# The gates' token sums made during the low-rank products, in a pool of their own

## The chip, the cores and the metric

The kernel runs on one core of a Trainium2 chip. Five engines work in parallel, each through its own list of instructions in a fixed order: PE (matmul), DVE (vector), ACT (activations and casts), POOL and SP (which here only issues DMAs). They wait for each other through semaphores. The metric is the device time of one execution in microseconds; of several runs the median is taken.

## The reference

One decoder layer, float32, 512 tokens, model width 1024. What matters here:

```python
h    = rms_norm(x, norm_g)
proj = h @ w_in     # HGRN2 q, f, i, z_a (1024 each) | c_q, c_kv, k_rope (704) | z_b | two gates (2048)
f    = lb + (1 - lb) * sigmoid(hf);  k = 1 - f;  log_f = log(f)
y_a  = rms_norm(hgrn2_recurrence(silu(hq), k, hi, log_f)) * silu(hz)
y_b  = mla(c_q, c_kv, k_rope) * silu(mz)
gates  = sigmoid(glog + b_gate)                      # glog: the last 2048 columns of proj
merged = gates[:, :, 0] * (y_a @ w_proj_a) + gates[:, :, 1] * (y_b @ w_proj_b)
out    = rms_norm(x + merged @ w_out)
```

## The kernel before, in words

**Split operands.** Every large product is computed from pairs: an operand is cut into a rounded part (`hi`, a cast on ACT, line 129) and the remainder (`lo`, a subtraction on DVE, line 130), and three matmuls (hi·hi, lines 102; hi·lo, 103; lo·hi, 104) take the place of one. `hT` is the normalised input, transposed, as such a pair: 8 blocks of 128 channels by 512 tokens.

**Weights.** `load_w` (line 110) brings 512 KB into one of three `w_raw` buffers by a DMA on SP's queue, then casts and subtracts into one of four `w_hi` and four `w_lo` buffers. Behind each of the early weight loads a second DMA is issued on the same queue (`queued`, line 124): copies of blocks of later weight matrices from DRAM to DRAM, named `g_t`, `pa_t` and `out_t` in the trace.

**The stages around the change.** First the input is normalised and transposed, with the first 256 columns of the low-rank product (lines 292 to 357, an order written out by hand). Then the other 448 columns: 96 matmuls over four token tiles (lines 394 to 400). These are the wide low-rank products of the change. Then the latent vectors are scaled and transposed into `cT` (lines 401 to 430), and four pairs of heads of the HGRN2 branch follow (`hg_pair`, line 582). A pair begins with `proj_ch` for the forget columns (48 matmuls into two accumulators in PSUM), `hg_forget` for both heads, and, in the even pairs, `proj_tok` for the values (96 matmuls, four accumulators). These accumulators, and those of the low-rank product, come from one ring of three PSUM buffers, `mm_ps`: a fourth can be started only when the first of the three has been read out.

`hg_forget` (line 456) reads its accumulator with a tanh on ACT (line 460, tile `tf`). From `tf` DVE makes `f` (461), POOL makes `k` and `fr` (463, 462), then DVE a scan (465), a reciprocal back into `tf`'s buffer (466) and a product `ki` (483).

**The token sums.** The two gates' products are later computed by a Strassen scheme of blocks, whose operands are sums of blocks of `hT` over tokens and channels. `early_sums(q)` (line 813) makes four such sums for half of the channel blocks: four additions hi + lo (line 820), four subtractions (773, 777), four splits (171 on ACT, 172 on DVE), and eight stores of 256 KB to DRAM (line 827), which POOL's queue reads back for the gates' products much later (line 1043). Each half is thus 12 instructions on DVE, 4 on ACT and 8 DMAs on SP's queue. Its tiles `qr`, `qs`, `qh`, `p3`, `qn`, `kn`, `qp` come from the pool `ma_pool`, one buffer each; `qn` is used twice in a half. The first half stands in the first pair behind `hg_forget`, the second behind that pair.

**What sets the order.** Outside the stretches marked `manual_schedule` a scheduler chooses each engine's order by its own estimate of times, so text that moves changes the order of other instructions too. The memory is a stack from the left and one from the right; a pool that was closed leaves its bytes to later pools, and an instruction that first writes such bytes waits until those who used them before are done, tile by tile (`reuse_waits="tile"`). `hpool` with `hT` is the left stack's bottom. `hgrn`, the pool of `hg_forget`'s tiles, is on the right stack and reaches down to the very end of `hpool`; `fr`, `gh`, `asb`, `tf`, `f`, `k`, `pr`, `ft`, `ki` are its lowest tiles, in this order.

Of the kernel before, what the change touches and what calls it, by code (L numbers as in the profile page):

```python
# [9 lines left out]
F32 = mybir.dt.float32  # L10
F32R = mybir.dt.float32r
# [3 lines left out]
ALU = mybir.AluOpType  # L15
# [3 lines left out]
P = 128  # L19
# [19 lines left out]
def hybrid_layer(ctx: ExitStack, tc: tile.TileContext, a):  # L39
    nc = tc.nc  # L40
# [11 lines left out]
    dram = ctx.enter_context(tc.tile_pool(name="dram", bufs=1, space=bass.MemoryType.DRAM))  # L52
# [116 lines left out]
    def split(hi, lo, src):  # L169

        nc.scalar.copy(hi, src)
        nc.vector.tensor_tensor(lo, src, hi.bitcast(F32), op=ALU.subtract)
# [34 lines left out]
    hT = [hpool.tile([P, KD, S], F32R, f"hT{i}") for i in range(2)]  # L207
# [181 lines left out]
    nc.vector.tensor_scalar(c1n[:], lb[:], 0.5, -0.5, op0=ALU.mult, op1=ALU.add)  # L389
    nc.vector.tensor_scalar(c2[:], lb[:], 0.5, 0.5, op0=ALU.mult, op1=ALU.add)  # L390

    for t2, ps in enumerate(c_ps):
        nc.scalar.copy(c_sb[:, 2 * t2 : 2 * t2 + 2, 0:256], ps[:].rearrange("p (t c) -> p t c", t=2))
    c_second += [load_c2(j) for j in range(2, 4)]
# [187 lines left out]
    def hg_pair(pair, in_forget=None, in_query=None, before_gate=None, last=None):  # L582
        cc, hs = pair * 256, (2 * pair, 2 * pair + 1)
        pf = proj_ch(w_in, COL_F + cc, hT)
        kk = [hg_forget(h, pf[i], None if i else in_forget) for i, h in enumerate(hs)]
        if pair:
            step()
        else:
            early_sums(kh[0])
        def gate():  # L590
            pz = proj_ch(w_in, COL_ZA + cc, hT)
            zz = [z_tile() for _ in hs]
            for i in range(2):
                silu2(zz[i][:], pz[i][:])
            return zz

        if pair % 2 == 0:
            for t in range(NT):
                v_sb[t] = hw.tile([P, 512], F32, f"v{t}")
            proj_tok(w_in, COL_I + cc, hT, lambda t, ps: nc.scalar.copy(v_sb[t][:], ps[:]))  # L600
        else:
            zz = gate()
        pq = proj_ch(w_in, COL_Q + cc, hT)
        qq = [hg_query(h, pq[i], kk[i][0], None if i else in_query) for i, h in enumerate(hs)]
        step()
        kts = [hg_turned(k[5]) for k in kk]
        sts = [hg_states(h, kts[i], kk[i][1], v_sb) for i, h in enumerate(hs)]
        if before_gate:
            before_gate()
        if pair % 2 == 0:  # L610
            zz = gate()
        def scores():
            return hg_scores([(h, kk[i][2:5] + qq[i][0:2]) for i, h in enumerate(hs)])

        def outs(aa):
            on = [hg_out(h, aa[i], sts[i], qq[i][2], v_sb) for i, h in enumerate(hs)]
            step()
            return on

        def gated(on):  # L620
            for i, h in enumerate(hs):
                hg_gate(h, on[i], zz[i])

        if last:
            return last(scores, outs, gated)
        gated(outs(scores()))
# [137 lines left out]
        nc.vector.tensor_tensor(yb[:, h], ops[:], z[:], op=ALU.mult)  # L764


    kh = [slice(0, 2), slice(2, 4)]
    half_t = [slice(0, 256), slice(256, 512)]
    blocks = lambda t: (t[:, 0:4, half_t[0]], t[:, 4:8, half_t[0]], t[:, 0:4, half_t[1]], t[:, 4:8, half_t[1]])
    TERMS = ((0, 0), (1, 1), (0, 1), (1, 0))  # L770

    def minus(out, x, y):
        nc.vector.tensor_tensor(out, x, y, op=ALU.subtract)

    def minus_minus(out, x, y):

        nc.vector.scalar_tensor_tensor(out, x, -1.0, y, op0=ALU.mult, op1=ALU.subtract)

    class BlockSums:

# [27 lines left out]
    gate_w = [BlockSums(f"g{b}", w_in[:, COL_G + b * D : COL_G + b * D + D]) for b in range(2)]  # L808
    pa_w = BlockSums("pa", a["w_proj_a"][0])
    out_w = BlockSums("out", a["w_out"][0])  # L810
    h_dram = [[dram.tile([P, 4, 256], F32, name=f"h{n}{i}") for i in range(2)] for n in range(1, 5)]

    def early_sums(q):

        E = lambda tag: ma_pool.tile([P, 2, 256], F32, tag)[:]
        h11, h12, h21, h22 = zip(*[[b[:, q] for b in blocks(t)] for t in hT])

        def whole(tag, hl):
            out = E(tag)
            nc.vector.tensor_tensor(out, hl[0].bitcast(F32), hl[1].bitcast(F32), op=ALU.add)  # L820
            return out

        def keep(n, tag, src):
            hl = Pair(ma_pool.tile([P, 2, 2, 256], F32R, tag)[:])
            split(*hl, src)
            for i in range(2):
                nc.sync.dma_start(h_dram[n - 1][i][:, q], hl[i].bitcast(F32))

        e22, e21, e11, e12 = whole("qr", h22), whole("qs", h21), whole("qh", h11), whole("p3", h12)
        minus(e22, e22, e21)  # L830
        keep(1, "qn", e22)
        minus_minus(e22, e22, e11)
        keep(2, "kn", e22)
        minus(e21, e11, e21)
        keep(3, "qp", e21)
        minus_minus(e12, e12, e22)
        keep(4, "qn", e12)

    adds = [(gate_w[0], 0), (gate_w[0], 2), (gate_w[1], 0), (gate_w[0], 1), (gate_w[1], 2), (gate_w[0], 3), (gate_w[1], 1),
            (pa_w, 0), (gate_w[1], 3), (pa_w, 2), None, (pa_w, 1), (out_w, 0), (pa_w, 3), (out_w, 2), (out_w, 1), (out_w, 3)]  # L840
# [1 line left out]
    def step():  # L842
        if adds and last_pool[0]:
            x = adds.pop(0)
            if x:
                x[0].add(x[1])
# [3 lines left out]

    for pair in range(H // 2 - 1):
        hg_pair(pair)
        if pair == 0:
            early_sums(kh[1])
    early = []

    def first_scores():
# [450 lines left out]
```

## Time and profile before

| | |
|---|---|
| median of 3 runs | 606.26 us (606.16 to 606.81) |
| the profiled execution, its own time | 606.53 us |
| its span, first to last instruction | 604.7 us |
| mean granted clock of PE | 0.996 |
| busy: PE, DVE, ACT, POOL | 595.2, 445.2, 283.0, 148.3 us |
| DMA | 115.34 MB, mean 191 GB/s |

A row of the time line gives start, duration, engine, line, operation, out<-in, shapes, count and, in brackets, the idle time ahead of it and what ended that. A row of the groups gives busy time and mean duration in ns behind the first bar, idle time behind the second. A matmul's row is longer than its share of PE, since matmuls overlap; the distance of two starts is what one costs.

### The profile page before, as it was taken

How to read it: one execution, taken by the hardware profiler on the slowest of the kernel's cores; microseconds unless marked ns; L12 is line 12 of the kernel's file. 1: busy time of each engine (PE TensorE's matmuls, PEld its weight loads, DVE VectorE, ACT ScalarE, POOL GpSimd, SP SyncE). 2: the span in 40 equal slices, each digit the busy share in tenths (PEclk: the TensorE clock that was granted, in tenths of full speed). 3: DMA queues.
4: the chain of work that ended last, by engine and by line, in shares of the span. 5: the costliest groups of instructions: out<-in, count | busy, mean ns of one | idle time of the engine just before them, and what ended most of it. 6: DMA issues, size and time to landing. Idle time of an engine off the chain costs nothing.

```text
span 604.7 us, 8828 instructions
## 1 busy us (share of the span) xinstructions
PE 595.2 (98%) x3198; PEld 501.5 (83%) x3198; DVE 445.2 (74%) x689; ACT 283.0 (47%) x517; POOL 148.3 (25%) x253
## 2 busy tenths in 40 slices
PE   9999999999999999999999999999999999999994
PEld 6998888888888888888888888888888888888883
DVE  7717989599764548959767776778878878466795
ACT  7555245333313342436545554456557764153553
POOL 3107322254350237415245540400000000000003
PEclk9999999999999999999999999999999999999998
DMA  8449479997969967582369676888666656366313
GB/s 281 159 137 345 155 220 370 318 223 169 239 152 253 232 194 155 112 186 76 62 153 175 147 159 154 222 289 244 192 187 204 204 182 188 123 233 257 102 36 139
DMA packets 73036, 115.34 MB, mean 191 GB/s; under 512 B 7561, under 2 KB 37663, under 8 KB 72993
## 3 DMA queue, kind: packets, MB, share of 16 engines
q1 hardware_dynamic: 63740, 90.99, 47.2%
q0 software_dynamic: 8336, 22.55, 20.2%
q10 hardware_dynamic: 916, 1.25, 0.6%
q8 instruction: 25, 0.41, 0.3%
q14 instruction: 19, 0.15, 0.1%
HBM read 106.38 MB, written 39.85 MB: 242 GB/s over the span
## 4 chain that ended last, share of the span: by engine, by line
PE 89%; DVE 4%; DMA 3%; ACT 2%; issue 1%; POOL 1%; SPq 0%; POOLq 0%; ACTq 0%; DVEq 0%
PE mm_ps L102 19%; PE mm_ps L104 19%; PE mm_ps L103 19%; PE ax_ps L889 16%; PE mm_ps L889 3%; PE ax_ps L754 1%; PE ax_ps L728 1%; DMA x<-x 1%; PE mm_ps L282 1%; PE ax_ps L556 1%; DVE ya L1173 1%; PE ax_ps L558 1%; PE ax_ps L518 1%; PE ax_ps L104 1%; PE ax_ps L103 1%
## 5 line engine op out<-in xcount | busy, mean ns | idle before, releaser
L130 DVE TENSOR_TENSOR w_lo<-w_raw,w_hi 128x1024 fp32r<-128x1024 f32 (+3 forms) x116 | 138.9, 1204 | 68.9 <-ACT w_hi L129 66.1
L129 ACT CAST w_hi<-w_raw 128x1024 fp32r<-128x1024 f32 (+3 forms) x116 | 114.8, 1007 | 132.6 <-PE mm_ps L103 54.7
L102 PE MATMUL mm_ps<-hT,w_hi 128*128 128x512 f32 x256 | 101.0, 395 | 0.0
L103 PE MATMUL mm_ps<-hT,w_hi 128*128 128x512 f32 x256 | 100.3, 392 | 0.0
L104 PE MATMUL mm_ps<-hT,w_lo 128*128 128x512 f32 x256 | 100.2, 393 | 0.0
L102 PE MATMUL mm_ps<-w_hi,hT 128*128 128x512 f32 (+1 forms) x160 | 61.7, 390 | 0.0
L103 PE MATMUL mm_ps<-w_lo,hT 128*128 128x512 f32 (+1 forms) x160 | 61.5, 385 | 0.0
L104 PE MATMUL mm_ps<-w_hi,hT 128*128 128x512 f32 (+1 forms) x160 | 61.4, 385 | 0.0
L104 PEld LDWEIGHTS mm_ps<-hT,w_lo 128*128 128x128 f32 x256 | 48.1, 188 | 9.9
L102 PEld LDWEIGHTS mm_ps<-hT,w_hi 128*128 128x128 f32 x256 | 48.1, 188 | 9.5
L103 PEld LDWEIGHTS mm_ps<-hT,w_hi 128*128 128x128 f32 x256 | 48.1, 188 | 9.4
L889 PE MATMUL ax_ps<-w_hi,s 128*128 128x512 f32 x208 | 51.5, 389 | 0.0
L889 PEld LDWEIGHTS ax_ps<-w_hi,s 128*128 128x128 f32 x208 | 39.0, 188 | 8.1
L1190 POOL TENSOR_SCALAR ssum<-ssum 128x1 f32<-128x1 f32 x3 | 0.7, 225 | 163.7 <-ACT z L1177 163.6
L104 PEld LDWEIGHTS mm_ps<-w_hi,hT 128*128 128x128 f32 x160 | 30.1, 188 | 5.5
L102 PEld LDWEIGHTS mm_ps<-w_hi,hT 128*128 128x128 f32 x160 | 30.0, 188 | 5.2
L103 PEld LDWEIGHTS mm_ps<-w_lo,hT 128*128 128x128 f32 x160 | 30.1, 188 | 5.1
L736 ACT ACTIVATE p<-ax_ps,sm 128x128 f32<-128x128 f32 (+3 forms) x32 | 16.8, 526 | 35.6 <-DVE sm L735 35.4
L738 POOL TENSOR_SCALAR p<-p,sm 128x128 f32<-128x128 f32 (+3 forms) x28 | 15.6, 563 | 65.0 <-DVE sm L737 54.3
L889 PE MATMUL ax_ps<-w_lo,s 128*128 128x512 f32 x104 | 27.8, 389 | 0.0
L466 DVE RECIPROCAL tf<-pr 128x512 f32<-128x512 f32 x8 | 26.8, 3348 | 0.1
L889 PEld LDWEIGHTS ax_ps<-w_lo,s 128*128 128x128 f32 x104 | 19.5, 188 | 4.0
(319 smaller groups left out, 1189.1 us busy)
## 6 DMA issues: line engine op xcount, KB each, us to landing
w_raw<-w_in SPq DMA_DIRECT2D x54, 512.0 KB, 7.0
g_t<-w_in SPq DMA_DIRECT2D x16, 512.0 KB, 8.9
w_raw<-g_t SPq DMA_DIRECT2D x16, 512.0 KB, 4.7
g_t<-w_in POOLq DMA_DIRECT2D x8, 512.0 KB, 10.5
pa_t<-w_proj_a SPq DMA_DIRECT2D x8, 512.0 KB, 8.4
g_t<-g_t POOLq DMA_DIRECT2D x8, 512.0 KB, 10.0
out_t<-w_out SPq DMA_DIRECT2D x8, 512.0 KB, 9.6
s<-h POOLq DMA_DIRECT2D x8, 512.0 KB, 11.7
```

Of the source, the lines that this page charges most:

```text
L102: nc.tensor.matmul(ps, lh[lsl], rh[rsl], start=start, stop=False)
L103: nc.tensor.matmul(ps, lh[lsl], rl[rsl], start=False, stop=False)
L104: nc.tensor.matmul(ps, ll[lsl], rh[rsl], start=False, stop=stop)
L129: last_hi[0] = nc.scalar.copy(hi[:, :o], raw[:, :o])
L130: last_lo[0] = nc.vector.tensor_tensor(lo[:, :o], raw[:, :o], hi[:, :o].bitcast(F32), op=ALU.subtract)
L282: nc.tensor.matmul(ps, hT[l][:, 4 * kh + k, t * P : t * P + P], c_hl[kh][r][:, k * 256 : k * 256 + 256], start=kh == 0 and kind == 0 and k ...
L466: nc.vector.reciprocal(rp[:], pr[:])
L518: nc.tensor.matmul(sps[:, sl], kt_[:, sl], v_sb[i][:, (h % 4) * P : (h % 4) * P + P], start=True, stop=True)
L556: nc.tensor.matmul(ops[:, sl], asb[:, sl], v_sb[i][:, (h % 4) * P : (h % 4) * P + P], start=True, stop=i == 0)
L736: last_act[0] = nc.scalar.activation(p[:, :n], sps[:, :n], AF.Exp, scale=SCALE, bias=sm[:, 1:2], accum_out=sm[:, 2:3])
L738: scaled_p = (nc.vector if final else nc.gpsimd).tensor_scalar(p[:, :n], p[:, :n], sm[:, 3:4], 0.5, op0=ALU.mult, op1=ALU.mult)
L889: nc.tensor.matmul(ps[:, o : o + n], ap[i][:, k, t * P : t * P + P], w[k // 2][j][:, k % 2, o : o + n], start=fresh and c == 0, stop=c == ...
```

## The change

`early_sums` is defined and called twice right behind the first, hand-ordered stage, ahead of the 448-column products, and its tiles come from a pool of its own, `ep`, of 20 KB per partition on the left stack. The pool is closed behind the two calls. `hg_pair` calls `step()` in pair 0 too, where it called `early_sums(kh[0])`; `step()` issues one of the additions on later weights (`adds`, two DMAs on POOL's queue), so each of these comes one step earlier than before. What the sums compute and what they store is the same.

```diff
@@ behind line 390
+    h_dram = [[dram.tile([P, 4, 256], F32, name=f"h{n}{i}") for i in range(2)] for n in range(1, 5)]
+
+    ep = Pool("early_sums", "left")
+    def early_sums(q):
+
+        E = lambda tag: ep.tile([P, 2, 256], F32, tag)[:]
...
+            hl = Pair(ep.tile([P, 2, 2, 256], F32R, tag)[:])
+            split(*hl, src)
+            for i in range(2):
+                nc.sync.dma_start(h_dram[n - 1][i][:, q], hl[i].bitcast(F32))
+
+        e22, e21, e11, e12 = whole("qr", h22), whole("qs", h21), whole("qh", h11), whole("p3", h12)
+        minus(e22, e22, e21)
+        keep(1, "qn", e22)
+        minus_minus(e22, e22, e11)
+        keep(2, "kn", e22)
+        minus(e21, e11, e21)
+        keep(3, "qp", e21)
+        minus_minus(e12, e12, e22)
+        keep(4, "qn", e12)
+
+    for q in kh:
+        early_sums(q)
+    ep.close()
     for t2, ps in enumerate(c_ps):
@@ hg_pair
-        if pair:
-            step()
-        else:
-            early_sums(kh[0])
+        step()
@@ behind the pool's old place
-        E = lambda tag: ma_pool.tile([P, 2, 256], F32, tag)[:]
...
     for pair in range(H // 2 - 1):
         hg_pair(pair)
-        if pair == 0:
-            early_sums(kh[1])
```

**Place 1: the first tanh on ACT, and SP's queue ahead of it.** `tf` (728 before, 796 now) is the tanh of the first head, `cT` and `kpe` are the latent vectors, `w_hi` casts of weights, `v0` the first value tile. In brackets stands for whose semaphore an instruction waits: DMAHW are counters of SP's DMAs. Before:

```order
L129 CAST w_hi_863<-w_raw_862 128x1024 [waits DMAHW3_49,DVE_49,PE_49]
L460 ACTIVATE tf_728<-mm_ps_664 128x512 [waits PE_49]
L423 ACTIVATE cT0_91<-ax_ps_578,par_399 128x512 [waits PE_49]
L423 ACTIVATE cT0_91<-ax_ps_585,par_399 128x512 [waits PE_49]
L423 ACTIVATE cT0_91<-ax_ps_592,par_399 128x512 [waits PE_49]
L423 ACTIVATE cT0_91<-ax_ps_599,par_399 128x512 [waits PE_49]
L423 ACTIVATE cT0_91<-ax_ps_606,par_399 128x512 [waits PE_49]
L129 CAST w_hi_882<-w_raw_881 128x1024 [waits DMAHW5_49,DVE_49,PE_49]
L171 CAST kpe_93<-ax_ps_613 128x512 [waits PE_49]
L460 ACTIVATE tf_757<-mm_ps_665 128x512 [waits DVE_49,Pool_49]
```

Now:

```order
L171 CAST qn_494<-p3_473 128x512 [waits DMAHW7_49,DMAHW4_49,DVE_49]
L129 CAST w_hi_920<-w_raw_919 128x1024 [waits DMAHW1_49,PE_49]
L466 ACTIVATE cT0_91<-ax_ps_654,par_399 128x512 [waits PE_49]
L466 ACTIVATE cT0_91<-ax_ps_661,par_399 128x512 [waits PE_49]
L466 ACTIVATE cT0_91<-ax_ps_668,par_399 128x512 [waits PE_49]
L466 ACTIVATE cT0_91<-ax_ps_675,par_399 128x512 [waits PE_49]
L466 ACTIVATE cT0_91<-ax_ps_682,par_399 128x512 [waits PE_49]
L171 CAST kpe_93<-ax_ps_689 128x512 [waits PE_49]
L503 ACTIVATE tf_796<-mm_ps_732 128x512 [waits DMAHW7_49,DMAHW2_49,DVE_49]
L640 COPY v0_856<-mm_ps_860 128x512 [waits PE_49]
L503 ACTIVATE tf_825<-mm_ps_733 128x512 [waits DVE_49,Pool_49]
```

The tanh has moved behind the five `cT` and behind `kpe`, and it waits for two DMAs: in the built program these counters stand for the two stores of `qn_494`, the last two rows `h40` and `h41` of SP's queue below. `tf_796` lies on bytes of `ep`'s `p3` and `qn`. SP's queue, now, up to the last of these stores:

```order
L420 DMA h11_425<-qn_476 128x512
L820 DMA g0_t3_718<-w_in 128x2x512
L123 DMA w_raw_919<-w_in 128x2x512
L820 DMA g0_t3_718<-w_in 128x2x512
L420 DMA h20_426<-kn_482 128x512
L123 DMA w_raw_994<-w_in 128x4x256
L820 DMA g0_t4_719<-w_in 128x2x512
L420 DMA h21_427<-kn_482 128x512
L420 DMA h40_430<-qn_494 128x512
L123 DMA w_raw_1001<-w_in 128x4x256
L820 DMA g0_t4_719<-w_in 128x2x512
L420 DMA h41_431<-qn_494 128x512
```

All sixteen stores stand between the weight loads of the first pair now; before, the first stood behind all weights of the first pair's forget, value and query products.

**Place 2: PE in the first value product.** `mm_ps` 822 and 823 (before), 860 and 861 (now) are the accumulators of the first two token tiles, the `w_hi` and `w_lo` the value weights in four pieces. Before, they take turns:

```order
L102 MATMUL mm_ps_822<-w_hi_825,hT0_125 128x512
L103 MATMUL mm_ps_822<-w_lo_826,hT0_125 128x512
L104 MATMUL mm_ps_822<-w_hi_825,hT1_126 128x512
L102 MATMUL mm_ps_823<-w_hi_825,hT0_125 128x512
L103 MATMUL mm_ps_823<-w_lo_826,hT0_125 128x512
L104 MATMUL mm_ps_823<-w_hi_825,hT1_126 128x512
```

Now the first is done whole, and the second waits for ACT:

```order
L102 MATMUL mm_ps_860<-w_hi_920,hT0_125 128x512
L471 MATMUL ax_ps_689<-ident_104,kd_639 128x128 [waits DVE_49,Pool_49]
L471 MATMUL ax_ps_689<-ident_104,kd_639 128x128 x3
L103 MATMUL mm_ps_860<-w_lo_921,hT0_125 128x512
L104 MATMUL mm_ps_860<-w_hi_920,hT1_126 128x512
L102 MATMUL mm_ps_861<-w_hi_863,hT0_125 128x512 [waits Activation_49]
L103 MATMUL mm_ps_861<-w_lo_864,hT0_125 128x512
```

All 24 matmuls of 860 stand ahead of the first of 861, which takes the ring buffer that the first tanh reads (`mm_ps_732`).

**Place 3: DVE behind the second head's reciprocal.** Now (`w_lo_996` is the first piece of the query weights, the `ki`, `pr`, `tf` with 8 in front are the two heads' tiles of `hg_forget`):

```order
L526 TENSOR_TENSOR ki_817<-k_798,tf_804 128x512
L527 TENSOR_TENSOR ko_818<-ki_817,pr_803 128x512
L504 TENSOR_SCALAR f_826<-tf_825,c1_418,c2_420 128x512
L529 TENSOR_TENSOR k128_819<-ko_818,gh0_708 128x512
L508 SCALAR_TENSOR_TENSOR pr_832<-f_826,fr_706 128x512
L509 RECIPROCAL tf_833<-pr_832 128x512
L526 TENSOR_TENSOR ki_846<-k_827,tf_833 128x512
L130 TENSOR_TENSOR w_lo_996<-w_raw_994,w_hi_995 128x1024
```

Before, eleven instructions of the sums and the subtraction for `kpe` stood among the same eight; none is left, and the query weight still stands behind the second head's `ki`.

More of the change, by code (lines that the diff above doesn't have):

```diff
@@ L390, in hybrid_layer, with minus, minus_minus, whole @@
     nc.vector.tensor_scalar(c2[:], lb[:], 0.5, 0.5, op0=ALU.mult, op1=ALU.add)
+    kh = [slice(0, 2), slice(2, 4)]
+    half_t = [slice(0, 256), slice(256, 512)]
+    blocks = lambda t: (t[:, 0:4, half_t[0]], t[:, 4:8, half_t[0]], t[:, 0:4, half_t[1]], t[:, 4:8, half_t[1]])
+    def minus(out, x, y):
+        nc.vector.tensor_tensor(out, x, y, op=ALU.subtract)
+    def minus_minus(out, x, y):
+        nc.vector.scalar_tensor_tensor(out, x, -1.0, y, op0=ALU.mult, op1=ALU.subtract)
+    h_dram = [[dram.tile([P, 4, 256], F32, name=f"h{n}{i}") for i in range(2)] for n in range(1, 5)]
+    ep = Pool("early_sums", "left")
+    def early_sums(q):
+        E = lambda tag: ep.tile([P, 2, 256], F32, tag)[:]
+        h11, h12, h21, h22 = zip(*[[b[:, q] for b in blocks(t)] for t in hT])
+        def whole(tag, hl):
+            out = E(tag)
+            nc.vector.tensor_tensor(out, hl[0].bitcast(F32), hl[1].bitcast(F32), op=ALU.add)
+            return out
+        def keep(n, tag, src):
+            hl = Pair(ep.tile([P, 2, 2, 256], F32R, tag)[:])
[14 more added lines that the diff above has]
+    ep.close()
     for t2, ps in enumerate(c_ps):
@@ L764, in mla_out @@
         nc.vector.tensor_tensor(yb[:, h], ops[:], z[:], op=ALU.mult)
-    kh = [slice(0, 2), slice(2, 4)]
-    half_t = [slice(0, 256), slice(256, 512)]
-    blocks = lambda t: (t[:, 0:4, half_t[0]], t[:, 4:8, half_t[0]], t[:, 0:4, half_t[1]], t[:, 4:8, half_t[1]])
     TERMS = ((0, 0), (1, 1), (0, 1), (1, 0))
[L772 to L777, printed above, removed]
     class BlockSums:
@@ L810, in hybrid_layer @@
     out_w = BlockSums("out", a["w_out"][0])
-    h_dram = [[dram.tile([P, 4, 256], F32, name=f"h{n}{i}") for i in range(2)] for n in range(1, 5)]
-    def early_sums(q):
-        E = lambda tag: ma_pool.tile([P, 2, 256], F32, tag)[:]
[L816 to L837, printed above, removed]
     adds = [(gate_w[0], 0), (gate_w[0], 2), (gate_w[1], 0), (gate_w[0], 1), (gate_w[1], 2), (gate_w[0], 3), (gate_w[1], 1),
```

## The prediction

> **What bounds the kernel now.** I read the share of busy time, then what PE waited for over the whole execution, then the time line of PE where the change acts.
>
> ```profile
> PE 595.2 (98%) x3198; PEld 501.5 (83%) x3198; DVE 445.2 (74%) x689; ACT 283.0 (47%) x517; POOL 148.3 (25%) x253
> PE ax_ps L247 <- DVE zero L293: 1.2, 1, 1.2
> PE ax_ps L271 <- DVE xn L263: 0.2, 1, 0.2
> PE ax_ps L889 <- DVE ya L1173: 0.2, 1, 0.2
> 44.52 0.39 PE L102 MATMUL mm_ps<-hT,w_hi 128*128 128x512 f32 x1
> 44.75 0.39 PE L103 MATMUL mm_ps<-hT,w_hi 128*128 128x512 f32 x1
> 53.82 2.34 PE L422 MATMUL ax_ps<-ident,c_sb 128*128 128x128 f32 x20
> 55.92 0.48 PE L104 MATMUL mm_ps<-hT,w_lo 128*128 128x512 f32 x1
> 57.63 0.39 PE L102 MATMUL mm_ps<-w_hi,hT 128*128 128x512 f32 x1
> 60.36 0.60 PE L428 MATMUL ax_ps<-ident,kd 128*128 128x128 f32 x4
> 60.72 0.48 PE L102 MATMUL mm_ps<-w_hi,hT 128*128 128x512 f32 x1
> ```
>
> The second to fourth row are all of PE's waits: 1.6 us in 604.7. Of its 9.5 us without work the rest lies ahead of the first matmul and behind the last. Two starts in a row are 0.23 us apart (44.52, 44.75). The 48 matmuls of the first forget product and the 20 transposes, from 44.52 to 57.63, take 13.11 us: 48 x 0.227 + 2.2. So PE is the bound, back to back. It follows that **nothing can be won**: the moved work stands on DVE, ACT and SP, and PE waits for none of them where it stood. The change can only keep PE fed or starve it, and each microsecond of starving arrives at the end whole, because no later wait of PE is there to swallow it.
>
> **The moved work itself.** Per half twelve instructions on DVE, four casts on ACT, eight stores.
>
> ```profile
> L820 DVE TENSOR_TENSOR qr<-hT,hT 128x512 f32<-128x512 f32 x2 | 1.4, 682 | 0.0
> L171 ACT CAST qn<-qr 128x512 fp32r<-128x512 f32 x2 | 1.2, 624 | 2.7 <-DMA h<-qn 1.5 <-DVE qr L773 1.2
> 42.40 1.23 DVE L130 TENSOR_TENSOR w_lo<-w_raw,w_hi 128x1024 fp32r<-128x1024 f32 x1 [12.16 <-ACT w_hi L129]
> 23.00:36.00 13.00, 13.00 (x71) 12.05 (x70) 5.09 (x17) 5.35 (x10) 0.00 (x0) 1.00 0.82 265
> 36.00:42.00 6.00, 6.00 (x31) 5.56 (x30) 0.00 (x0) 4.03 (x13) 0.00 (x0) 1.00 0.08 31
> ```
>
> The last two rows are stretches: length, busy time of PE, PEld, DVE, ACT and POOL, granted clock, busy share of the DMA engines, GB/s. 24 x 0.68 = 16.4 us on DVE and 8 x 0.62 = 5.0 us on ACT leave the first pair, where they cost nothing, and come to these stretches, where DVE has 7.9 and 6.0 us free; some 2.5 us run over into the next. PE's matmuls are 0.19 us apart there (31 in 6.00 us); the first that needs a delayed `w_lo` is the fortieth, about 7.5 us after their start, and that `w_lo` gets five sums, 3.4 us, ahead of it on DVE. So I take 0 here. Of the forget product's first `w_lo` I am less sure. DVE began it at 42.40; two more casts stand ahead on ACT (1.2 us), so it ends at 43.6 + 1.26 = 44.9, and the fifth matmul needs it at 44.52 + 4 x 0.227 = 45.4. Bound: 0 to 0.7, taken 0. The additions that come one step earlier are DMAs of POOL's queue behind the forget work, past the place that decides, taken 0.
>
> **Where it starves PE: the first tanh.** In the new pool the sums' tiles lie on the bytes of the first head's tiles, and the built program has the tanh wait for the last two stores. While the tanh waits, its accumulator is not read; the ring has three buffers, so the second accumulator of the value product (861) cannot start; PE stands there, since it works in order.
>
> *When PE comes there.* The forget product now runs through: 44.52 + 48 x 0.227 = 55.4; 20 transposes 2.2: 57.6; 24 matmuls of the first accumulator 5.45 and four transposes 0.36 (60.36 to 60.72): **63.4**.
>
> *When the tanh can start.* First, ACT works in order and `kpe` stands ahead.
>
> ```profile
> 52.88 0.60 ACT L460 ACTIVATE tf<-mm_ps 128x512 f32<-128x512 f32 x1 [0.47 <-PE mm_ps L104]
> 61.00 0.59 ACT L171 CAST kpe<-ax_ps 128x512 fp32r<-128x512 f32 x1 [2.35 <-PE ax_ps L428]
> 50.72 2.61 DVE L418 TENSOR_SCALAR c_sb<-c_sb,css 128x384 f32<-128x384 f32 x8 [0.93 <-POOL css L177]
> 49.82 0.37 SPq L123 DMA_DIRECT2D w_raw<-w_in  x1
> 50.24 0.56 SPq L790 DMA_DIRECT2D g_t<-w_in  x1
> h<-qn SPq DMA_DIRECT2D x1, 256.0 KB, 2.0
> h<-qp SPq DMA_DIRECT2D x2, 256.0 KB, 8.4
> h<-kn SPq DMA_DIRECT2D x2, 256.0 KB, 10.7
> 43.00:58.00 15.00, 15.00 (x79) 12.88 (x78) 10.52 (x17) 9.06 (x16) 9.49 (x18) 1.00 0.91 295
> 87.00:105.00 18.00, 18.00 (x115) 14.93 (x113) 15.84 (x25) 7.92 (x12) 3.78 (x4) 1.00 1.07 371
> ```
>
> Its four transposes end at 57.6 + 22 x 0.227 + 0.6 = 63.2, the cast at 63.8: even with all stores done PE waits until 64.4, **1.0 us**. Second, the stores. I bound the landing of the last one from two sides.
>
> By issue and landing: on SP's queue it stands behind a weight load that needs the third value weight's `lo`. DVE makes that after scaling `c_sb`, which ended at 53.3 and, with two sum casts ahead on ACT, ends about 1.5 us later; plus 1.2 for the `lo`: 56; a load and a copy are issued ahead (0.4 and 0.6): the store is issued at about 57.3. On an idle queue a store of 256 KB landed 2.0 us after its issue (the window 70 to 72), on a full one 8.4 (94 to 96) and 10.7 us (100 to 104). That is 59.3 at the least, and **65.7 to 68.0** if the queue is full.
>
> It is full: the window from 43 to 58 had the DMA engines 91% busy with ten transfers of 512 KB; these stay, and six stores and the table that POOL loads (512 KB) come among them. By bytes: from 45.1, when the second value weight can be issued (its buffer is free when the forget product's first `lo` is done, at 44.9), 11 x 512 + 6 x 256 KB = 7.34 MB stand up to and with that store. At 371 GB/s, the rate of the full stretch in the last row, 19.8 us, at the 295 of the other row 24.9; plus the 1.3 us that a lone store takes beyond its 0.7 us of transfer: 66.2 to 71.3. I take **67.5**, where both ways overlap. Then the tanh ends at 68.1 and PE starts at 68.2: **4.8 us** of standing (bounds 1.0 and 71.3 + 0.7 - 63.4 = 8.6).
>
> [...]
>
> **What is late next.** The tanh begins the chain of both heads, and at its end stands the `lo` of the query weight.
>
> ```profile
> L130 DVE TENSOR_TENSOR w_lo<-w_raw,w_hi 128x1024 fp32r<-128x1024 f32 x17 | 21.1, 1257 | 18.7 <-ACT w_hi L129 18.7
> L466 DVE RECIPROCAL tf<-pr 128x512 f32<-128x512 f32 x3 | 10.0, 3343 | 0.0
> L463 POOL TENSOR_SCALAR k<-tf,c1n,c 128x512 f32<-128x512 f32 x3 | 5.7, 1914 | 8.4 <-ACT tf L460 8.4
> L465 DVE TENSOR_TENSOR_SCAN pr<-f,fr 128x512 f32<-128x512 f32 x3 | 3.7, 1220 | 1.1 <-POOL fr L462 1.1
> L462 POOL TENSOR_SCALAR fr<-f 128x16 f32<-128x16 f32 x3 | 2.0, 682 | 0.2
> L483 DVE TENSOR_TENSOR ki<-k,tf 128x512 f32<-128x512 f32 x3 | 2.0, 682 | 0.0
> ```
>
> A head: tanh 0.60, `k` 1.91 and `fr` 0.68 on POOL, scan 1.22, reciprocal 3.34, `ki` 0.68: 8.4 us; the second tanh writes the same buffer and waits for the first `ki`. Two heads and the `lo` 1.2: 18.1, with a dozen handovers of some 0.05 about 18.7 after the first tanh starts. PE needs that `lo` after the rest of the value product (72 x 0.227 = 16.3), three transposes 0.3 and two matmuls 0.5, all from 0.7 after the tanh's start: 17.8. PE stands another **0.8** (bounds 0 and 1.5), whenever the first tanh decided PE's start.
>
> The sum: 4.8 + 0.8 = 5.6 us. The profiled execution took 606.53; 612.1 for such a one, and 606.26 + 5.6 = 611.9 by the median: **612.0**.
>
> **The rivals.**
>
> *The clock falls in the pause.* For it: the pause of 4.8 us, and that PE's matmuls on zeros at the start, after standing, have a mean of 515 ns where the 512-column ones have 395 later.
>
> ```profile
> L247 PE MATMUL ax_ps<-zero 128*128 128x512 bf16 x17 | 6.5, 515 | 1.2 <-DVE zero L293 1.2
> 1.18 3.17 PE L247 MATMUL ax_ps<-zero 128*128 128x512 bf16 x7 [1.18 <-DVE zero L293]
> ```
>
> There seven take 3.17 us, 0.45 each, double the 0.23. If PE runs at half its pace for as long as it stood, 4.8 us, it loses 2.4, and the second stall is covered: 606.3 + 4.8 + 2.4 = **613.5**. Against it: the granted clock never falls in the rows above, and the pause may be too short. [...]
>
> *The stores land early.* If the queue has room (the window 36 to 42 shows 8% busy, so that a backlog may be gone), the last store lands before 64 and only `kpe` and the second stall stay: 1.0 + 0.8 = 1.8, **608.1**. Against it: 7.34 MB from 45.1 would have to move at over 400 GB/s; no window here shows that.
>
> *Not slower.* The stores are early and the chain of the heads, now free of eleven sums on DVE, ends 0.8 us earlier than I add it up; then only `kpe`'s 1.0 us stays: **607.2**, within 0.2%. It decides from a landing before 63.8 on. For faster speaks only the emptier DVE of the first pair; PE did not wait for DVE there.
>
> **How the numbers follow.** Forecast 0.57, clock 0.20, early stores 0.14, not slower 0.09 (of it 0.02 faster). 0.2%, or 1.2 us, is what a measurement here tells from no change. Slower 0.91, same 0.07, faster 0.02. The range leaves out no more than 2 in 10: from 608.6 (stores at 64.2, 1.5 + 0.8) to 615.0 (stores at 69.0 and the slow clock, 6.3 + 2.4).
>
> **What will show it.** In PE's waits a new row, first accumulator of the value product's second tile behind ACT's tanh, 3 to 6 us once, at 63 to 69 us, and ahead of the tanh the store of `qn` as its releaser; a second of about 1 us for `w_lo` near 86. In the windows, PE idle there and nowhere else, and from then on each stage later by one amount. Wrong if PE has no idle time around 64 us, if the pause ends with something other than the tanh, or if PE's idle time and the loss differ by over 1 us; then the clock or a stall that I did not see carries the rest.

## The result, and the profile after

The changed kernel takes **615.86 us** (median of five executions, 615.22 to 617.45), the kernel before, measured beside it, 606.64. The ratio is 1.0156, 95% interval 1.0145 to 1.0168: slower by 9.2 us.

The profiled execution is the slowest of the five (617.45 us, span 615.6). Its busy shares:

```profile
PE 599.6 (97%) x3198; PEld 502.9 (82%) x3198; DVE 447.7 (73%) x689; ACT 282.0 (46%) x517; POOL 147.3 (24%) x253
```

The shares have hardly moved: PE's fell from 98% to 97%, although the program got 1.6% longer, since matmuls at half clock count as busy (6.94 of the 7.00 us from 71 to 78 us, at a mean clock of 0.56). The two longest of PE's new waits (us in total, times, longest); two more are a wait of 0.3 us at 9 us, ahead of the moved work, and 0.4 us in place of 0.2 at the end, at L890:

```profile
PE mm_ps L102 <- ACT tf L503: 5.5, 1, 5.5
PE ax_ps L465 <- DVE c_sb L461: 0.6, 1, 0.6
```

The first wait is the one that was forecast: PE stands in front of an accumulator until the first tanh has read another. The second is new and was not forecast: transposes of `c_sb` that wait for its scaling. The stretches around the pause (length, busy time of PE, PEld, DVE, ACT, POOL, granted clock, busy share of the DMA engines, GB/s):

```profile
66.00:71.00 5.00, 0.00 (x0) 0.00 (x0) 0.48 (x1) 0.59 (x2) 0.00 (x0) 0.93 1.03 380
71.00:78.00 7.00, 6.94 (x18) 5.49 (x19) 5.89 (x5) 0.49 (x3) 2.67 (x11) 0.56 0.08 30
```

PE does nothing for the whole of the first stretch. In the second it is busy without a break and starts 18 matmuls where the kernel before started 32 in the same seven microseconds: the granted clock is 0.56. Both belong to the loss, and only one is idle time.

To see where the 10.9 us between the two profiled executions lie, I took for each matmul how much later it starts after the one before it than matmuls of its shape usually do, and added that up by place:

| place in the changed kernel | us lost against before |
|---|---|
| start, to 20 us | 0.2 |
| first matmuls of the forget product, 45 to 46 us | 0.6 |
| transposes of `c_sb`, 57 to 59 us | 1.1 |
| the pause in front of the tanh, 65.4 to 71.1 us | 5.6 |
| matmuls at half clock, 71.1 to 77.1 us | 2.9 |
| 80 to 120 us | 0.25 |
| the last 30 us | 0.3 |

That is 10.95, and the last matmul starts 10.95 us later (607.65 against 596.70). Nothing is left over.

What the pause consists of, from the time lines of ACT, SP's queue and DVE:

```profile
65.17 0.59 ACT L171 CAST kpe<-ax_ps 128x512 fp32r<-128x512 f32 x1 [2.90 <-PE ax_ps L471]
70.41 0.60 ACT L503 ACTIVATE tf<-mm_ps 128x512 f32<-128x512 f32 x1 [4.66 <-DMA h<-qn]
...
60.03 0.38 SPq L123 DMA_DIRECT2D w_raw<-w_in  x1
60.47 0.64 SPq L820 DMA_DIRECT2D g_t<-w_in  x1
61.30 0.87 SPq L420 DMA_DIRECT2D h<-qn  x1
...
55.04 3.83 DVE L461 TENSOR_SCALAR c_sb<-c_sb,css 128x384 f32<-128x384 f32 x8 [1.88 <-POOL css L177]
58.79 1.21 DVE L130 TENSOR_TENSOR w_lo<-w_raw,w_hi 128x1024 fp32r<-128x1024 f32 x1
```

Read from the bottom: the scaling of `c_sb` ends at 58.87 instead of 53.33; the `lo` of the third value weight follows it and frees the buffer for the load at 60.03; behind that load and a copy the last store is issued at 61.30; it lands at 70.3, and the tanh, which had nothing else to wait for since 65.8, starts. The chain is the one of the prediction, later at its beginning.

Why `c_sb` is scaled so late stands on ACT and POOL. First the kernel before, then the change:

```profile
44.72 0.54 ACT L400 COPY c_sb<-mm_ps 128x448 f32<-128x448 f32 x1 [0.16 <-PE mm_ps L104]
45.33 1.17 POOL L411 TENSOR_TENSOR kd<-c_sb,ktab 128x256 f32<-128x256 f32 x1 [27.80 <-ACT c_sb L400]
46.47 0.45 POOL L412 TENSOR_TENSOR kt<-c_sb,ktab 128x128 f32<-128x128 f32 x1
47.43 0.47 POOL L176 TENSOR_SCALAR css<-css 128x4 f32<-128x4 f32 x2
```

```profile
47.13 0.53 ACT L443 COPY c_sb<-mm_ps 128x448 f32<-128x448 f32 x1
47.74 1.80 POOL L454 TENSOR_TENSOR kd<-c_sb,ktab 128x256 f32<-128x256 f32 x1 [31.54 <-ACT c_sb L443]
49.50 0.91 POOL L455 TENSOR_TENSOR kt<-c_sb,ktab 128x128 f32<-128x128 f32 x1
51.37 1.84 POOL L176 TENSOR_SCALAR css<-css 128x4 f32<-128x4 f32 x2
```

The last copy of `c_sb` starts 2.4 us later: ACT works without a break from 40.45 us up to it, and casts of the sums stand between the weights' casts and squares that were there before. From the copy's start to the start of the scaling POOL then takes 7.9 us instead of 6.0, since the same instructions last up to twice as long (0.91 for 0.45), or four times (1.84 for 0.47), while DVE works on sums and `lo` parts beside them. (The first of the powers behind them, L177, took 1.0 us less than before; the 1.9 us are the balance.) And the scaling itself takes 3.83 us for 2.61. That is 2.4 + 1.9 + 1.2 = 5.5 us.

### The profile page after: what moved, and what is told of

Same layout as the page of the kernel before. It is cut to its first block, busy times and chain, and to the rows that moved or that the text cites. A ratio compares the mean times of both kernels' runs of the same rounds, so it can differ in the third digit from the quotient of the medians.

```text
span 615.6 us, 8832 instructions
## 1 busy us (share of the span) xinstructions
PE 599.6 (97%) x3198; PEld 502.9 (82%) x3198; DVE 447.7 (73%) x689; ACT 282.0 (46%) x517; POOL 147.3 (24%) x253
## 4 chain that ended last, share of the span: by engine, by line
PE 77%; DMA 8%; DVE 6%; ACT 3%; issue 3%; POOL 1%; SPq 0%; POOLq 0%; ACTq 0%; DVEq 0%
PE ax_ps L890 16%; PE mm_ps L102 15%; PE mm_ps L104 15%; PE mm_ps L103 15%; DMA w_raw<-w_in 4%; DMA h<-qn 3%; PE mm_ps L890 3%; DVE w_lo L130 2%; PE ax_ps L794 1%; PE ax_ps L768 1%; ACT w_hi L129 1%; DMA x<-x 1%; PE ax_ps L599 1%; DVE ya L1174 1%; PE ax_ps L601 1%
## 5 line engine op out<-in xcount | busy, mean ns | idle before, releaser
L102 PE MATMUL mm_ps<-w_hi,hT 128*128 128x512 f32 (+1 forms) x160 | 63.3, 399 | 5.5 <-ACT tf L503 5.5
L103 PE MATMUL mm_ps<-w_lo,hT 128*128 128x512 f32 (+1 forms) x160 | 62.8, 392 | 0.0
L104 PE MATMUL mm_ps<-w_hi,hT 128*128 128x512 f32 (+1 forms) x160 | 62.5, 391 | 0.0
L890 PE MATMUL ax_ps<-w_hi,s 128*128 128x512 f32 x208 | 51.4, 389 | 0.0
L890 PEld LDWEIGHTS ax_ps<-w_hi,s 128*128 128x128 f32 x208 | 39.0, 188 | 8.0
L102 PEld LDWEIGHTS mm_ps<-w_hi,hT 128*128 128x128 f32 x160 | 30.7, 192 | 11.4 <-ACT tf L503 5.9
L104 PEld LDWEIGHTS mm_ps<-w_hi,hT 128*128 128x128 f32 x160 | 30.8, 192 | 5.9
L890 PE MATMUL ax_ps<-w_lo,s 128*128 128x512 f32 x104 | 27.8, 389 | 0.0
L890 PEld LDWEIGHTS ax_ps<-w_lo,s 128*128 128x128 f32 x104 | 19.5, 188 | 4.1
```

Of the source, the lines that this page charges most:

```text
L102: nc.tensor.matmul(ps, lh[lsl], rh[rsl], start=start, stop=False)
L103: nc.tensor.matmul(ps, lh[lsl], rl[rsl], start=False, stop=False)
L104: nc.tensor.matmul(ps, ll[lsl], rh[rsl], start=False, stop=stop)
L890: nc.tensor.matmul(ps[:, o : o + n], ap[i][:, k, t * P : t * P + P], w[k // 2][j][:, k % 2, o : o + n], start=fresh and c == 0, stop=c == ...
```

## The experiments

**Take the wait away, leave all work where the change put it.** A pad moves the sums' tiles off the first head's bytes.

```diff
-    ep = Pool("early_sums", "left")
+    ep = Pool("early_sums", "left"); ep.tile([P, 9216], F32, "below")
```

> The sums' tiles are lifted by 36 KB per partition, off every byte that the first head's tanh, scan and products write; every engine's order and all moved work stay as they are. Theory (the loss of 9.2 us comes from the tanh's wait for the last stores, 5.6 us, and from the slow clock after it, 2.9 us): both vanish. What stays is a pause of 1.0 to 1.2 us behind the cast of kpe, the 0.8 us of the query weight's lo that the slow clock had covered, and 1.6 us of small gaps between 44 and 59 us: 609 to 610 us, the granted clock 1.00 throughout. Rival (the heads are late anyway because the moved sums and casts delay DVE and ACT): the pause in front of the tanh stays above 3 us and the time above 612. Rival (nothing but the store counts): 606.3 to 607.

Measured: 611.68 us (610.23 to 613.59), ratio 1.0084 (1.0059 to 1.0110), profiled 613.59. PE's waits from 50 us on (another of 1.4 us, at 9 us, stands ahead of all moved work):

```profile
PE ax_ps L561 <- ACT kt L553: 2.8, 1, 2.8
PE mm_ps L102 <- ACT tf L503: 0.7, 1, 0.7
PE ax_ps L465 <- DVE c_sb L461: 0.5, 1, 0.5
```

The pause in front of the tanh is 0.7 us, and the clock stays at 1.00 behind it. Every engine keeps its order, so the shared bytes are the only difference to the changed kernel, and the wait for the stores is shown. Both rivals fall: the heads are not late by themselves, and the stores are not all. But the theory's 609 to 610 us at full clock throughout was missed as well, and the first row is a wait that nobody had named: at 100.6 us PE needs the second head's `kt`, which stands on ACT behind the cast of a weight that has not landed. The chain of waits has it (start, us, what), and the windows below it show what the DMA engines did, first the padded kernel, then the kernel before in the same stretch:

```profile
87.28 14.21 DMA w_raw<-w_in
```

```profile
92.00:96.00 4.00, 4.00 (x24) 3.43 (x23) 2.47 (x3) 1.55 (x2) 0.00 (x0) 1.00 1.11 224
```

```profile
92.00:96.00 4.00, 4.00 (x22) 3.38 (x21) 3.88 (x7) 1.95 (x3) 0.47 (x1) 1.00 1.08 369
```

The weight took 14.2 us to land; the engines are as busy in both (1.11 and 1.08), and move 224 instead of 369 GB/s. What differs there is the change's other edit: the first two accumulating transfers, which add a block of weights onto a block in DRAM, issued by POOL at 85.5 us and not at 100.9.

**Is the half clock a consequence of the pause?** Idle products, whose result nobody reads, fill the pause from its front: 24, 12 or 6 of them.

```diff
     split(*kpe, ps[:])
+    filler = ax_tile()
+    for _ in range(24): nc.tensor.matmul(filler[:], hT[0][:, 0, 0:P], hT[0][:, 0, :], start=True, stop=True)
```

> The changed kernel with 24 idle products (5.5 us of PE) put in front of the accumulator that waits for the tanh, into a spare bank that nobody reads. Theory (the half clock after the pause is a consequence of PE standing still): PE stands for under 0.5 us, the granted clock stays 1.00 from 71 to 77 us, the 2.9 us are won back, and the query weight's lo, no longer covered, costs about 0.8: 613 to 614 us against 615.9. Rival (the slow stretch is a throttle that comes from the full DMA queue, or comes by time and not from standing): the clock is 0.50 after 71 us all the same and the time is 615.5 to 616.5.

> As the kernel with 24 idle products, with 12 of them: PE works 2.7 us of the 5.6 and stands for 2.9. Theory A (the clock falls only after a pause of some fixed length between 2.9 and 5.6 us): no slow stretch, 613 to 614 us. Theory B (PE runs at half pace for as long as it stood): 2.9 us of standing cost 1.4 us more, 614 to 615. Rival (any pause over 1 us brings the full slow stretch of 5.7 us): 615.5 to 616.5.

> As before with 6 idle products: PE works 1.4 us and stands for about 4.3. Theory A (a fixed length of pause, above which the clock falls for a fixed time): if 4.3 us are enough, the slow stretch is as long as after 5.6 us (5.7 us, 2.9 us lost) and the time is 615.5 to 616; if not, 613 to 614. Theory B (half pace for as long as it stood): a slow stretch of 4.3 us, 2.1 us lost, 614.8 to 615.3.

Measured: 615.11 us (613.73 to 615.51), 615.09 (614.12 to 616.20) and 615.12 (613.32 to 615.97). The times hardly differ; the profiles do. With 24 the pause is gone, the clock is 1.00 in every stretch from 64 to 79 us, and of the 2.9 us won PE loses 1.9 again, at the place that the pad had laid bare. That wait, and the stretch in which the pause would have been:

```profile
PE ax_ps L561 <- ACT kt L553: 1.7, 1, 1.7
```

```profile
64.00:68.00 4.00, 4.00 (x19) 3.30 (x18) 0.69 (x1) 0.26 (x1) 0.00 (x0) 1.00 1.06 390
```

So standing still is the cause of the half clock, not the full queue: the DMA engines are as full as in the changed kernel (1.06 at 390 GB/s), and the tanh, behind `kpe`, still waits 3.8 us for the store, until 68.05. This rests on one profile, of the quickest of four executions (613.73). The three others took 615.1 to 615.5, as long as with fewer idle products, and have no profile; their mean clocks, 0.993 to 0.997, don't tell whether it fell in them, since executions of the kernel before, which has no pause, show 0.995 to 0.998. By the median the forecast of 613 to 614 was missed. For the length of the half clock I read its edges from narrow windows. One row is one window of 3.41 us; the column behind POOL's is the clock. The changed kernel, PE idle from 65.4 to 71.1:

```profile
66.88:70.29 3.41, 0.00 (x0) 0.00 (x0) 0.00 (x0) 0.00 (x0) 0.00 (x0) 1.00 1.05 386
70.29:73.70 3.41, 2.64 (x6) 2.15 (x7) 1.69 (x2) 1.07 (x2) 1.32 (x2) 0.50 0.33 127
73.70:77.12 3.42, 3.42 (x9) 2.64 (x8) 3.39 (x2) 0.00 (x0) 1.36 (x9) 0.50 0.01 2
```

Six idle products, PE idle from 66.3 to 71.2:

```profile
65.17:68.58 3.41, 1.32 (x6) 0.75 (x4) 0.69 (x1) 0.09 (x1) 0.00 (x0) 1.00 1.07 391
68.58:71.99 3.41, 0.83 (x2) 0.73 (x3) 0.55 (x1) 1.08 (x2) 0.76 (x1) 0.50 0.69 259
71.99:75.41 3.42, 3.42 (x9) 2.65 (x9) 2.72 (x2) 0.00 (x0) 1.91 (x11) 0.50 0.02 7
```

Twelve, PE idle from 68.0 to 70.7:

```profile
68.80:72.21 3.41, 1.51 (x7) 1.24 (x8) 0.55 (x2) 1.07 (x2) 1.32 (x2) 1.00 0.73 271
72.21:75.63 3.42, 3.42 (x10) 2.64 (x9) 3.39 (x2) 0.00 (x0) 1.35 (x9) 0.50 0.01 2
```

The half clock came in pieces of 3.41 us, one or two of them, and what decided was the piece before: idle for all of it in the changed kernel, for 61% with six, for 56% with twelve. With twelve the clock falls 1.5 us *after* PE has begun to work again. A piece in which PE was busy throughout (3.42 of 3.42 us in all three) brought the full clock back; one with PE idle for 23% of it (70.29 to 73.70) did not. So neither theory of mine holds as written: not a fixed length of pause, and not half pace for as long as PE stood, though the median with six lies in the range that the second one gave. The price of a pause was 1.7 us, half of 3.41, for each such piece that fell on work: 1.6 us with twelve, 2.1 with six (one piece lies mostly in the pause), 2.9 in the changed kernel.

**The early additions alone.** In the kernel before, only `step()` is moved ahead.

```diff
-        if pair:
-            step()
-        else:
+        step()
+        if pair == 0:
             early_sums(kh[0])
```

> The kernel before, with one part of the change alone: the first additions to the weight sums (two accumulating transfers on POOL's queue) are put out behind the first pair's forget work instead of behind its query work; the gates' sums stay where they were. The padded kernel showed a weight that took 14.2 us to land (87.28 to 101.49) while these two were under way, against 7.4 us before, and PE waiting 2.9 us for what stood behind it on ACT. Theory (the early additions take the place of the weights in the DMA engines): here too a weight of the first pair lands late and PE waits 1.5 to 3 us between 95 and 106 us: 608 to 610. Rival, and the prediction's own figure (they cost nothing): 606.3 to 607.0, no new wait of PE.

Measured: 610.66 us (610.09 to 611.42), ratio 1.0063 (1.0051 to 1.0075). The prediction's figure of nothing falls; the price of the edit is 3.9 us. The place is another than I expected. PE's waits, then ACT's longest wait between 90 and 125 us, then a stretch of it:

```profile
PE ax_ps L572 <- DVE k L564: 2.6, 2, 2.0
PE mm_ps L102 <- ACT tf L460: 0.9, 1, 0.9
```

```profile
ACT qn L171 <- DMA h<-qn: 11.6, 1, 11.6
```

```profile
96.00:100.00 4.00, 4.00 (x22) 3.38 (x21) 4.00 (x8) 0.15 (x1) 1.19 (x3) 1.00 1.11 244
```

The kernel before in the same stretch:

```profile
96.00:100.00 4.00, 4.00 (x23) 3.37 (x22) 4.00 (x7) 1.49 (x3) 0.26 (x1) 1.00 1.07 383
```

Again a full queue that moves a third less. Here it is a store of the sums' second half that lands late; ACT's next cast of the sums writes the same buffer and waits 11.6 us, the heads' squares stand behind that cast, and PE waits at 121.7, 124.9 and 135.6 us (2.2, 0.7 and 1.0). The transfers are not alone in this price: with the moved text the scheduler also changed other orders, and on SP's queue both stores of that `qn` now stand behind a weight load and a copy, where the first had stood ahead of them. The padded kernel with and without the early additions, next, is the cleaner pair.

**The padded kernel with late additions**, in three profiles. The edit puts every addition back by the one step:

```diff
-        step()
+        step() if pair else None
```

> The padded kernel, with the first additions back behind the query work. Every engine but POOL keeps its order. Theory (the padded kernel's rest of 5.1 us is 2.9 us of waiting for the weight that the early additions delay, 1.6 us of slow clock after that pause, and small waits): the wait near 100 us and the slow clock behind it go, 0.9 us in front of the accumulator that waits for the tanh and about 0.9 us in front of the transposes of c_sb stay, and so does the wait for the query weight's lo if it is real (0.8 us): 608 to 609. Rival (the heads' chain is late by itself): PE waits about 2 to 3 us near 100 us all the same, 610.5 to 612.

> The padded kernel with late additions once more, for one further profile: its first profiled execution took 607.7 us and showed 1.5 us of waits, while the median of its six executions was 609.7. If the profile falls on an execution of the upper group, PE shows a further wait of about 2 us, most likely near 100 us for the weight that is late in some executions; if on one of the lower group, the waits are 1.5 us again.

> The padded kernel with late additions a third time, for one more profile. Two profiles took 607.7 and 607.9 us with 1.5 us of waits, four further executions 609.3 to 610.3. If this one is of the upper group, its profile shows where the 2 us lie: PE waiting near 100 us, or slower matmuls without a wait. If it is of the lower group, the waits are 1.5 us as before and the upper group stays unexplained.

Measured: 609.68 us (607.70 to 610.28), ratio 1.0039 (1.0025 to 1.0053); the single executions 607.90 and 608.97. In the first profile (607.70):

```profile
PE mm_ps L102 <- ACT tf L503: 0.7, 1, 0.7
PE ax_ps L465 <- DVE c_sb L461: 0.4, 1, 0.4
```

The wait near 100 us and the half clock behind it are gone, as the theory has it, and the rival falls. Only POOL's order differs from the padded kernel's, so the early additions are the cause; the weight that took 14.2 us there lands in 6.6 here (85.88 to 92.48). Their price is 2.0 us by the medians, which stands beside the unexplained part below. The 0.8 us for the query weight's `lo` do not appear, though nothing covers them here. The third profile (608.97) has 0.2 us more in front of the transposes and 1.0 us at the end of the kernel, at L890. Four of the six executions took 609.3 to 610.3, above the 608 to 609 that the theory gave, and no profile fell on one of those: their last microsecond stays unexplained.

**The changed kernel with late additions**, the same edit without the pad:

> The changed kernel, with the first additions back behind the query work and all else as it is. Theory (in the changed kernel the 5.6 us of pause and 2.9 us of slow clock put PE so far behind that it does not notice the late weight): no difference, 615.4 to 616.4. Rival (the early additions are a part of the loss of the changed kernel): 613 to 614.

Measured: 615.24 us (612.91 to 615.81), ratio 1.0125 (1.0107 to 1.0142). PE's first wait in it:

```profile
PE mm_ps L102 <- ACT tf L503: 6.2, 1, 6.2
```

By the medians 0.6 us below the changed kernel, by the ratios 0.3%; the profiled execution (615.81) has the pause and the half clock (2.4 us) and no sign of the additions, like the changed kernel's own, which lost 0.25 us between 80 and 120. What the additions cost alone is hidden here behind a loss that comes earlier; whether all of it, these runs can't tell.

**ACT's order.** The padded kernel with late additions, and the cast of `kpe` behind the two tanhs.

```diff
-    split(*kpe, ps[:])
+    kpe_ps = ps
...
+    def late_kpe():
+        with tc.issue_after(last_act[0].ins): split(*kpe, kpe_ps[:])
...
-        nc.scalar.activation(tf[:], pf[:], AF.Tanh, scale=0.5)
+        last_act[0] = nc.scalar.activation(tf[:], pf[:], AF.Tanh, scale=0.5)
...
-        step() if pair else None
+        step() if pair else late_kpe()
```

> The padded kernel with late additions, with the cast of kpe put behind the two tanhs of the first pair; nothing else in the order of PE, POOL or SP changes. Theory (the 0.9 us in front of the accumulator that waits for the tanh come from ACT's order alone: the tanh stands behind the cast): that wait is gone, the time 0.9 us below that of the kernel with the cast ahead: 606.8 us for the quickest execution, a median of 608.8 or less. Rival (the tanh waits for something else as well): the wait stays above 0.5 us and the time is the same.

Measured: 607.54 us (606.62 to 609.63), ratio 1.0012 (1.0000 to 1.0024). ACT's rows:

```profile
61.39 0.62 ACT L503 ACTIVATE tf<-mm_ps 128x512 f32<-128x512 f32 x1
71.32 0.58 ACT L171 CAST kpe<-ax_ps 128x512 fp32r<-128x512 f32 x1
```

The tanh starts at 61.39, three microseconds before PE needs its accumulator, and the wait is gone: `kpe` was all of it. What is left of the loss is 0.8 us in front of the transposes of `c_sb`.

**Half of the move.** First half early, second half where the first stood.

```diff
-    for q in kh:
-        early_sums(q)
+    early_sums(kh[0])
     ep.close()
...
-        step()
+        step() if pair else early_sums(kh[1], ma_pool)
```

> Half of the move: the first half of the sums beside the low-rank products, in the padded pool, the second half behind the first pair's forget work where the first half stood, the first additions behind the query work. Theory (the scaling of c_sb is late because twelve further sums and four casts stand ahead of it): it ends at most 1 us later than in the kernel before, PE's waits in front of the transposes are under 0.2 us, and the first tanh, with no stores to wait for and ahead of kpe's cast, costs nothing: 606.3 to 607.2. Rival (any part of the sums beside the low-rank products delays it): waits of 0.5 us or more at 55 to 60 us, 607.5 to 608.5.

Measured: 607.03 us (606.03 to 609.04), ratio 1.0005 (0.9995 to 1.0015): no difference. Its only new wait, and the scaling of `c_sb`:

```profile
PE mm_ps L104 <- DVE w_lo L130: 0.4, 1, 0.4
```

```profile
51.17 2.60 DVE L461 TENSOR_SCALAR c_sb<-c_sb,css 128x384 f32<-128x384 f32 x8 [0.93 <-POOL css L177]
```

With half of the sums the scaling starts 0.45 us later than before and the transposes don't wait. The stretch of the low-rank products has room for one half, not for two. None of these kernels is quicker than the kernel before.

**Late by issue, or by a full engine?** The last two stores go out on POOL's queue.

```diff
-                nc.sync.dma_start(h_dram[n - 1][i][:, q], hl[i].bitcast(F32))
+                (nc.gpsimd if n == 4 and q == kh[1] else nc.sync).dma_start(h_dram[n - 1][i][:, q], hl[i].bitcast(F32))
```

> The changed kernel, with the last two stores of the sums (the two for which the first tanh waits) put out on POOL's queue, which is idle there, ahead of the table, instead of on SP's queue behind a weight load. Theory A (the store is late because it is issued late, at 61.3, and stands behind what the queue had taken before): on a queue of its own it is issued at about 61 and lands 2 to 4 us later, PE's pause falls to 1 to 2 us, the clock stays at 1.00, but the wait behind the early additions, no longer covered, comes near 100 us as in the padded kernel: 610 to 612. Theory B (the DMA engines themselves are full, whatever queue): it lands 7 us or more after its issue, the pause stays above 4 us: 614.5 to 616.5.

Measured: 611.16 us (610.06 to 611.29), ratio 1.0067 (1.0048 to 1.0085). The store, the tanh that waits for it, and the windows of the pause:

```profile
59.34 0.55 POOL L420 DMA_DIRECT2D h<-qn  x1 [1.81 <-DVE qn L172]
65.73 0.60 ACT L503 ACTIVATE tf<-mm_ps 128x512 f32<-128x512 f32 x1 [1.04 <-DMA h<-qn]
```

```profile
64.37:67.78 3.41, 1.56 (x7) 1.18 (x7) 1.24 (x2) 1.40 (x3) 1.25 (x2) 1.00 1.05 394
67.78:71.18 3.40, 3.40 (x10) 2.62 (x9) 3.26 (x2) 0.00 (x0) 1.43 (x10) 0.50 0.74 276
```

Issued 2.0 us earlier, the store lands in 6.4 us instead of 9.0: both theories have a part. Freed of its place in SP's queue it gains 4.6 us in all, but with the engines full (394 GB/s) it doesn't land in the 2 to 4 us that I gave it. The pause is 2.0 us, and even that brings one piece of half clock, against theory A; the wait near 100 us, no longer covered, came with 0.6 us.

## Why the prediction was right, and where it was wrong

The direction and the pause were forecast rightly. What failed is what the sum put at nothing: the clock behind the pause, 2.9 us, and the moved work ahead of it, 1.7 us.

*PE is back to back, and each microsecond of starving arrives whole.* Right for the changed kernel: the table's delays add up to the whole of the difference between the profiled executions. But "no later wait of PE is there to swallow it" does not hold: the early additions made one near 100 us, which the pause hid, so that taking the pause away gave back less than it had cost. The direction followed from this, and no kernel of the study went below the one before.

*The first tanh waits for the last stores, through tiles that share bytes.* Right in mechanism: the tanh's releaser is the store, and with tiles elsewhere the pause falls to 0.7 us.

*PE arrives at 63.4.* It came at 65.4. Of these 2.0 us 0.2 are from the start, 0.6 from the forget product (inside its bound of 0 to 0.7, taken as 0) and 1.1 from the transposes.

*The moved work at 0.* This is the step that failed first. I had DVE's and ACT's free time in the stretches, and the `lo` products in view, and gave the scaling of `c_sb` a delay of 1.5 us that no one on PE would notice; it was 5.5, and the transposes waited. The order on ACT had 2.4 us of it, and POOL, which I had not looked at, 1.9.

*The last store issued at 57.3, landing at 67.5.* Issued at 61.3, for the reason just given, landing at 70.3. My bound by bytes (66.2 to 71.3) held; the bound by issue (65.7 to 68.0) was built on the early scaling, and I chose the value where the two overlap. The **4.8 us of pause** measured 5.6, less wrong than its parts by luck: PE came 2.0 us late and the store 2.8.

*The clock.* The largest error, and the step that failed most: the forecast took the full clock behind the pause. The fall of the clock was a rival at 0.20 and 2.4 us; it came, and cost 2.9. The working of the forecast allowed only PE's idle time, and its own test said what it would mean if loss and idle time differ: here by 2.9 us at the pause. I held the pause to be perhaps too short, which no row of the kernel before showed; 2.0 us was enough in the kernel with stores on POOL's queue. The price "half pace for as long as it stood" came near for a wrong reason.

*0.8 us for the query weight's `lo`.* Did not come, and was not merely covered: the padded kernel with late additions doesn't have it either. The chain of the two heads was shorter than I made it, 17.7 us from the tanh's start (70.41) to the end of that `lo` (88.08) in place of 18.7, because `k` and `fr` of the first head took 1.03 and 0.29 us on POOL with DVE mostly idle beside them, where I had put the means 1.91 and 0.68 from a stretch in which DVE was full of sums. In the second head `k` took 1.55, and `fr` stood behind another product of POOL (0.62).

*The additions one step earlier at 0.* Wrong by itself: 3.9 us in the kernel before (with the orders that changed there), 2.0 in the padded one. In the changed kernel most or all of it is hidden, so the term did little harm to the time; but "past the place that decides" was a statement on PE's waits alone, and the cost runs through the DMA engines to weights and stores 10 to 30 us later.

Put together: 5.6 + 0.8 was forecast as 4.8 + 0.8 with all else at nothing; measured are 5.6 for the pause, 2.9 for the clock, 1.7 for the moved work ahead of it, 0 for the `lo`. That is 10.2 of the 10.9 us by which the profiled executions differ; the medians, 9.2 apart, stand a little lower. The pause's 0.8 us too little and the `lo`'s 0.8 too much cancel, which is luck; the two terms set at nothing, 4.6 us together, are what is missing between 612.0 and 615.9. *Early stores* and *not slower* fell with the landing at 70.3.

## What to carry to other kernels

Before work is moved into an engine's free time, follow each in-order chain of that stretch to the engine that bounds the kernel, through the engines that receive no work as well: here ACT's order, a POOL that was slow beside a working DVE and a longer scaling made `c_sb` 5.5 us late, while all busy shares had room. Tiles in a reused piece of memory hand the next stage a wait for their *last store*, and on full DMA engines that was 6 to 9 us behind its issue (6.4 on POOL's queue, 9.0 on SP's); another place for the tiles takes it away without touching the order. A pause of PE is to be priced with the clock behind it, and a wait that disappears is to be followed by the question which later one it had covered: undoing the pause here laid bare a wait of 2.9 us behind a transfer that the same change had moved.

## What the runs showed of the hardware

**The clock.** In eight profiled pauses of PE the granted clock fell to 0.50 for one or two pieces of 3.4 us, or not at all. Pauses of 2.0 (stores on POOL's queue), 2.7 (twelve idle products) and 2.9 us (padded kernel) brought one piece, of 4.8 (six), 5.6 (changed kernel) and 6.4 (the same with late additions) two; pauses of 1.9 (24 idle products) and 2.2 us (early additions alone) brought none. So the length alone doesn't decide. In the clock records of the two kernels the pieces lie on a grid of 3.413 us: in the changed kernel 19 of them from the first record to the fall (5.44 to 70.29), two at half clock (to 77.12) and 157 to the next fall (613.01); in the kernel before 174 from the first record to the one fall, behind the last matmul (6.07 to 599.99). A pause counted by its share of a piece, and the piece did not have to be idle throughout. Half clock followed pieces in which PE was idle for all of it (changed kernel, 66.88 to 70.29 and 609.60 to 613.01), for 88% (the end of the kernel before, 596.57 to 599.99), 81% (padded kernel), 61% (six idle products), 56% (twelve) and 54% (stores on POOL's queue). It did not follow pieces idle for 37% and 49% (changed kernel, 63.46 to 66.88 and 606.18 to 609.60), nor the 2.2 us with early additions alone, which fell across two pieces, idle for 51% and 25%; and of the pause with 24 idle products PE's rows leave 1.74 us without a matmul, 51% of a piece at the most. Matmuls' ends are modelled, so the border between 51% and 54% is rough. First the fuller piece of the early additions; then the padded kernel, whose pause of 2.9 us ended at 103.5, half a microsecond before the clock fell:

```profile
120.42:123.84 3.42, 1.69 (x8) 1.07 (x6) 1.65 (x2) 3.20 (x18) 1.44 (x3) 1.00 1.01 372
```

```profile
100.62:104.03 3.41, 0.66 (x5) 0.48 (x5) 1.36 (x3) 2.09 (x4) 0.00 (x0) 1.00 1.07 372
104.03:107.44 3.41, 3.41 (x12) 2.83 (x11) 3.31 (x9) 0.87 (x1) 1.81 (x3) 0.50 1.01 346
```

**POOL beside DVE.** The same 128x128 multiplication took 0.45 us on POOL beside an idle DVE (the kernel before, and the one with half of the move) and 0.91 us beside one that was working on sums. It goes the other way too: the first power of `css` took 2.01 us in the kernel before, with a `lo` on DVE for part of it, and 1.03 in the changed kernel, with DVE idle. In both pairs of rows the price was a factor of two. That this alone made POOL slow was not tried by itself.

**Accumulating transfers.** While the additions ran, the DMA engines were 1.11 busy and moved 224 (padded kernel, 92 to 96 us) and 244 GB/s (early additions alone, 96 to 100); in the same stretches of the kernel before they moved 369 and 383 at 1.08 and 1.07. In the padded kernel a weight beside them took 14.2 us to land, against 6.6 with the additions put back.
